# A second timetable for the attention stage of a two-layer trunk: shares, merge, gate, weight splits and loads set to other steps, dense rounds 14 steps on

## The chip, the cores and the metric

The kernel runs on one core of one Trainium2 chip. The metric is device microseconds of one launch, the median of several runs. One more execution was taken with the hardware profiler; all rows of the trace come from it. Engines are named as in the profile: PE (TensorE), DVE (VectorE), ACT (ScalarE), POOL (GpSimd), SP (SyncE, which here only issues DMAs).

## The reference, cut to what matters

Two layers on x (1024 tokens by 1024 channels, float32). Layer 0 is a gated short convolution. Layer 1, which the change is in, is an attention with 16 heads of 64 channels in three dilation groups:

```python
proj = h @ w_in                                   # q, k, v of 3 groups, and z
for g, (window, dilation) in enumerate(((128, 1), (512, 4), (2048, 16))):
    q, k = rms_norm(q), rms_norm(k)
    o, l = dilated_group_attention(q, k, v, bias_g, window, dilation)   # l = log of the softmax's sum
alpha = softmax(stack(lses), axis=0)              # shares of the three groups, per token and head
o = sum(alpha[..., None] * stack(outs))           # merge
y = o * silu(z)                                   # gate
return x + y @ w_out                              # dense
```

## The kernel before, in words

The first four fifths of the span make layer 0 and the projections of layer 1; they write q and k (`qkd`), v (`vd`), silu(z) (`zd`) and the residual (`x1d`) to DRAM. The change does not touch them. The last stage reads these back and works through 24 units: a pair of heads `hp` (0 to 7) by a group `g` (0 to 2).

A unit has 4 steps (g = 0 and 1) or 2 (g = 2), so a pair has 10 and the stage has 80. The last step of pair hp is step 10·hp + 9. The order on each engine is written out by hand: all five engines are under a manual schedule, so each does its instructions in the order in which the Python code issues them. `attention(hp, g)` gives each step a table from lag to pieces of work, and the loop at the end runs, at step k, the pieces of lag 0 of step k, of lag 1 of step k−1, and so on:

- lag 0, `A`: PE scores into two of three PSUM banks, then on DVE bias and row minimum (L935), which frees the banks. `E` (end of the step): ACT exponentials.
- lag 2, `B`: PE transposes (L948), copies from PSUM to `pts` on DVE or ACT.
- lag 4, `C`: PE products with V (L969, L962); when a unit is through, DVE copies the sum to `o` (L984, and L981 for g = 2).
- `store`: minimum and sum of each row go to DRAM (`nld`, L993 and L996) from the POOL queue; for g = 2, `ml` reads the values of the other two groups back (L991), also from POOL, after `nld` has landed.
- For g = 2 of a pair, lags from its last step: `weights` (2) and `shares` (3) on DVE, with one small exponential on ACT; `store_shares` and `spread` (3) send them through DRAM and back, broadcast, into `fb` and `sqacc` (POOL queue); `scale` (8, 9, 10): three 128x1024 products on DVE (L1035); `add` (9, 10): two 128x1024 sums on POOL (L1038); `gate` (12) on DVE (L1041); `high` (12) on ACT and `low` (13) on DVE (L1048) split the result into two float32r parts.

Pair 7 has an ending of its own, which the change leaves as it is.

The output product is done in rounds of two pairs. A round has 16 tiles (8 row blocks by 2 halves of the tokens); a tile is six matmuls of 128x512 (L1129 to L1131) into one bank `pd`, and at the start of the next step DVE adds the bank to `acc` (L1165). One tile goes into one step, at its end. Round r (0 to 2) begins at step 20·(r+1) + LD, with LD = 13; what is left at step 80 goes in pairs into the steps after it. Its weights are read by `fetch` (SP), split by `split` (ACT, L1140) and `split_low` (DVE, L1143). In this text a dense step is one that has such a tile, a plain step one that has none.

Loads for a unit are issued on SP six steps ahead (bias, q, k) and two steps ahead (V). silu(z) of a pair (`sz`, two buffers) is loaded with q and k of g = 2, at step 10·hp + 2. The 16 `residual` loads (256 KB each) fill `acc` at steps 27 to 42.

Of the kernel before, what the change touches and what calls it, by code (L numbers as in the profile page):

```python
# [10 lines left out]
F32 = mybir.dt.float32  # L11
# [8 lines left out]
P = 128  # L20
D = 1024
S = 1024
# [6 lines left out]
HP = H // 2  # L29
# [6 lines left out]
def trunk(ctx: ExitStack, tc: tile.TileContext, a, out):  # L36
    nc = tc.nc
# [60 lines left out]
    def spread(hf, src, pool):  # L98
        cs = slice(hf * HALF, hf * HALF + HALF)
        pb = pool.tile([P, HALF], F32, name="st", tag="st")  # L100
        for j in range(4):
            b = hf * 4 + j
            nc.tensor.transpose(pb[:, j * P:(j + 1) * P], src[:, b:b + 1].to_broadcast([P, P]), ident)
        if src is rtok:
            nc.scalar.activation(R1[:, cs], pb, AF.Copy)
        else:
            mt = ftile()
            mc = mt.rearrange("p (c q) -> p c q", q=32)
            nc.vector.transpose(mc, pb.rearrange("p (c q) -> p c q", q=32))
            nc.vector.tensor_scalar(er2[:, hf * 16:(hf + 1) * 16], mc[:, :, 0], 8.0 * EPS, None, op0=OP.mult)  # L110
# [9 lines left out]
    zd = dram.tile([HP, P, S], F32, name="zd")  # L120
# [14 lines left out]
    with tc.tile_pool(name="wq", bufs=1) as wq, tc.tile_pool(name="sle", bufs=1) as sle, \  # L135
# [11 lines left out]
        def ftile():  # L147
            t = fp.tile([P, HALF], F32, name="f", tag="f", bufs=12)
            return t
# [185 lines left out]
        with tc.tile_pool(name="rp", bufs=1, side="right") as rp, tc.tile_pool(name="cp", bufs=2, side="right") as cp, \  # L335
# [3 lines left out]
            VB, US, TS, SZ = {}, {}, {}, {}  # L339
# [475 lines left out]
    with tc.tile_pool(name="sp", bufs=1, space=PSUM) as sp, tc.tile_pool(name="ptp", bufs=2, space=PSUM) as ptp, \  # L815
# [11 lines left out]
        QK, VS, SZ, y2, part = {}, {}, {}, {}, {}  # L827
        acc = [ap.tile([P, S], F32, name="acc", tag=f"acc{dt}", bufs=1) for dt in range(KT)]

        def loads(hp, g):  # L830
            QK[hp, g] = [ap.tile([P, S], F32, name="qk", tag="qk", bufs=6) for _ in range(2)]
            for i in range(2):
                nc.sync.dma_start(QK[hp, g][i], qkd[hp, g, i])
            if g == 2:
                SZ[hp] = ap.tile([P, S], F32, name="sz", tag="sz", bufs=2)
                nc.sync.dma_start(SZ[hp], zd[hp])

        def load_v(hp, g):
            VS[hp, g] = ap.tile([P, 8, P], F32, name="V", tag="V", bufs=3)
# [23 lines left out]
        def attention(hp, g):  # L863
# [165 lines left out]
            def spread(w):  # L1029
                fb = u["fb", w] = fbp.tile([P, S], F32, name="fb", tag="fb") if w else sqacc  # L1030
                for s, hs in enumerate((lo, up)):
                    nc.gpsimd.dma_start(fb[hs], fd[hp, w, s][None, :].to_broadcast([64, S]))

            def scale(w):
                nc.vector.tensor_tensor(O[hp, w], O[hp, w], u["fb", w], op=OP.mult)  # L1035

            def add(w):
                nc.gpsimd.tensor_tensor(O[hp, 1], O[hp, 1], O[hp, w], op=OP.add)  # L1038
# [22 lines left out]
            def spread_last(hf):  # L1061

                b0, b1, b2 = (scores().rearrange("p a b -> p (a b)") for _ in range(3))
                for w in (2, 1):
                    for r in range(8):
                        for a, b in enumerate((b0, b1)):
                            hs = slice(64 * a + 32 * hf, 64 * a + 32 * hf + 32)
                            nc.tensor.transpose(b.rearrange("p (w i r) -> p w r i", w=2, r=8)[:, w - 1, r],
                                                u["wide", w][hs, r * P:r * P + P], ident[hs, hs])
                mine = ident.rearrange("p (a h i) -> p h a i", a=2, h=2)[:, hf]  # L1070
                for r in range(8):
                    nc.tensor.matmul(b2.rearrange("p (i a r) -> p r a i", a=2, r=8)[:, r],
                                     u["wide", 0][:, r * P:r * P + P], mine, start=True, stop=True)
                u["fb", 0] = b2
                for w in (2, 1):
                    u["fb", w] = [b.rearrange("p (w i r) -> p w i r", w=2, r=8)[:, w - 1] for b in (b0, b1)]

            def last(hf, i):
                h, z = half(hf), SZ[hp][:, half(hf)]
                if i == 0:  # L1080
                    for w in (2, 1):
                        for a, b in enumerate(u["fb", w]):
                            o = O[hp, w][:, h].rearrange("p (i a r) -> p a i r", a=2, r=8)[:, a]
                            nc.vector.tensor_tensor(o, o, b, op=OP.mult)
                    nc.vector.tensor_tensor(O[hp, 0][:, h], O[hp, 0][:, h], u["fb", 0], op=OP.mult)
                elif i == 1:
                    for w in (2, 0):
                        nc.vector.tensor_tensor(O[hp, 1][:, h], O[hp, 1][:, h], O[hp, w][:, h], op=OP.add)
                    nc.vector.tensor_tensor(z, O[hp, 1][:, h], z, op=OP.mult)
                    if hf == 0:  # L1090
                        y2[hp] = [ap.tile([P, S], F32R, name="qk", tag="qk", bufs=6) for _ in range(2)]
                    nc.scalar.activation(y2[hp][0][:, h], z, AF.Copy)
                else:
                    nc.vector.tensor_tensor(y2[hp][1][:, h], z, y2[hp][0][:, h].bitcast(F32), op=OP.subtract)

            steps = []
# [7 lines left out]
            if g == 2:  # L1104
                if hp == HP - 1:
                    steps[-2][3] = steps[-2].pop(LC)
                    end[3] = end.pop(LC)
                    todo = [(2, shares), (2, wide), (3, lambda: spread_last(0)), (3, lambda: last(0, 0)),
                            (3, lambda: last(0, 1))]
                    ending.update(turn=end.pop(LB)[0], weights=weights, spread=spread_last, last=last)  # L1110
                else:
                    todo = [(LB, weights), (3, shares), (3, store_shares), (3, lambda: spread(2)),
                            (3, lambda: spread(1)), (3, lambda: spread(0)), (8, lambda: scale(2)),
                            (9, lambda: scale(1)), (9, lambda: add(2)), (10, lambda: scale(0)),
                            (10, lambda: add(0)), (12, gate), (12, high), (13, low)]
                for lag, f in todo:
                    end.setdefault(lag, []).append(f)
            return steps, prefetch

        LB, LC = 2, 4  # L1120
        LD = 13
        W, ending = {}, {}

        def dense(ps, kts, dt, hf, first, last):
# [37 lines left out]
        def add_sums():  # L1162
            while sums:
                ps, x = sums.pop(0)
                nc.vector.tensor_tensor(x, ps, x, op=OP.add)  # L1165

        steps, at = [], {}
        for un in units:
            st, prefetch = attention(*un)
            at[un] = len(steps), prefetch  # L1170
            steps += st
        begins, extra = {}, {}
        for un, (k, prefetch) in at.items():
            begins.setdefault(max(-1, k - 6), []).extend([prefetch, lambda un=un: loads(*un)])
        tiles = [(dt, hf) for hf in range(2) for dt in range(KT)]

        def when(k, f, *x):
            begins.setdefault(k, []).append(lambda: f(*x))

        for un, (k, prefetch) in at.items():  # L1180
            when(max(0, k - 2), load_v, *un)
        for i, (dt, hf) in enumerate(tiles):
            when(27 + i, residual, dt, hf)
        for r in range(3):
            k0 = at[2 * r + 2, 0][0] + LD
            k = k0
            for i, (dt, hf) in enumerate(tiles):
                late = k >= len(steps)
                name = "pd" if not late else (("pd", "ps"), ("pd", "ps"), ("pd", "pt"), ("pt", "pd"))[
                    min(k - len(steps), 3)][i % 2]  # L1190
                if i >= 14:
                    name = "po"
# [1 line left out]
                                               some((2 * r, 2 * r + 1), dt, hf, name))  # L1194
                k += (i % 2 if i < 13 else 0) if late else 1
        for kt in range(KT):
            k = at[kt // 2 * 2 + 2, 0][0] + LD - 4 + kt % 2 if kt < 6 else len(steps) - 5 + kt % 2
            when(k - 4 - kt % 2, fetch, kt)
            when(k, split, kt)
            when(k + 1, split_low, kt)  # L1200
        when(len(steps), ending["turn"])
        when(len(steps), ending["weights"])
        for f in begins.pop(-1):
# [1 line left out]
        k = 0  # L1205
        while k < len(steps) + LC - 1 or any(x >= k for x in extra):
            add_sums()
            for lag in (0, 1, LC, 3, *range(LC + 1, 15), LB):
                for f in steps[k - lag].get(lag, ()) if 0 <= k - lag < len(steps) else ():
                    f()  # L1210
            for f in steps[k].get("exps", ()) if k < len(steps) else ():
                f()
            for f in extra.get(k, ()):
                f()
            for f in begins.get(k, ()):
                f()
            k += 1
# [94 lines left out]
```

## Time and profile before

| | |
|---|---|
| median of 3 runs | 1976.92 us (1972.67 to 1980.83) |
| the profiled execution, its own time | 1979.19 us |
| its span in the trace | 1977.4 us |
| mean granted clock of TensorE | 0.989 |
| PE busy | 1919.6 us (97%) |
| DVE busy | 1494.7 us (76%) |
| ACT busy | 886.0 us (45%) |
| POOL busy | 847.3 us (43%) |

Busy shares are of the whole span. The attention stage has its first scores at about 1629 us and ends with the span; shares within it are read from windows.

### The profile page before, as it was taken

The numbers are of one execution on the slowest core, as the hardware profiler recorded it, in microseconds if no ns is written. First come the engines' busy times: TensorE is split into PE (matmuls) and PEld (weight loads), VectorE is DVE, ScalarE is ACT, GpSimd is POOL, SyncE is SP. The second block draws the span as 40 slices with busy tenths as digits, with TensorE's granted clock in tenths as the row PEclk, the third lists the DMA queues.
The fourth block names the chain that finished last, engine by engine and source line by source line (L and its number), as shares of the span: only waits on it lengthen the run. The fifth ranks groups of instructions, "written<-read, shape, count | busy, mean of one in ns | idle before, by whom it ended". The sixth has DMA issues, their size and how long they took to land.

```text
span 1977.4 us, 30596 instructions
## 1 busy us (share of the span) xinstructions
PE 1919.6 (97%) x10894; PEld 1558.5 (79%) x10894; DVE 1494.7 (76%) x2769; ACT 886.0 (45%) x2031; POOL 847.3 (43%) x767
## 2 busy tenths in 40 slices
PE   8999999999999999999999999999999998899988
PEld 6888888888888888878877888788888876576767
DVE  6866766666666555798889689868988867888896
ACT  6433333333334453444343443434334338877770
POOL 0366667766665211334434444444434342323330
PEclk9999999999999999999999999999999998998999
DMA  6312232222324575413233232323233257888742
GB/s 192 121 57 88 86 107 75 96 90 82 94 67 158 179 239 165 141 67 122 92 117 118 72 120 103 121 75 128 86 107 107 101 176 226 235 260 237 204 138 86
DMA packets 116777, 253.79 MB, mean 128 GB/s; under 512 B 17598, under 2 KB 22814, under 8 KB 116624
## 3 DMA queue, kind: packets, MB, share of 16 engines
q1 hardware_dynamic: 93280, 176.89, 28.2%
q0 software_dynamic: 23344, 74.95, 11.2%
q8 instruction: 85, 1.39, 0.3%
q14 instruction: 68, 0.56, 0.1%
HBM read 192.53 MB, written 67.64 MB: 132 GB/s over the span
## 4 chain that ended last, share of the span: by engine, by line
PE 77%; DVE 12%; issue 4%; ACT 3%; DMA 3%; POOL 1%; SPq 0%; DVEq 0%; POOLq 0%; ACTq 0%
PE pp L301 17%; PE pp L304 17%; PE pp L303 17%; PE pp L552 3%; PE pp L553 3%; PE pp L551 3%; PE pt L948 3%; DVE ws L165 2%; PE po L969 2%; DVE blkc L716 2%; PE pp L374 1%; PE pp L375 1%; PE pp L376 1%; ACT xs L941 1%; DMA nld<-nl 1%
## 5 line engine op out<-in xcount | busy, mean ns | idle before, releaser
L165 DVE TENSOR_TENSOR ws<-wr,ws 128x512 fp32r<-128x512 f32 x284 | 280.4, 989 | 122.0 <-ACT ws L164 120.6
L164 ACT ACTIVATE ws<-wr 128x512 fp32r<-128x512 f32 x284 | 178.3, 629 | 357.8 <-PE pp L304 232.7
L164 ACT ACTIVATE ws<-sr 128x512 fp32r<-128x512 f32 x272 | 169.9, 629 | 296.5 <-PE pp L304 235.9
L276 POOL TENSOR_TENSOR sr<-wr 128x512 f32<-128x512 f32 x136 | 185.8, 1366 | 261.3 <-DMA wr<-in_wqk 82.9
L165 DVE TENSOR_TENSOR ws<-sr,ws 128x512 fp32r<-128x512 f32 x272 | 225.8, 838 | 72.0 <-ACT ws L164 69.7
L313 DVE TENSOR_TENSOR f<-pp,f 128x512 f32<-128x512 f32 x204 | 139.8, 685 | 92.3 <-PE pp L304 85.6
L941 ACT ACTIVATE xs<-xs,nl 128x256 f32<-128x256 f32 (+2 forms) x384 | 160.3, 423 | 0.7 <-DVE nl L935 0.7
L309 ACT ACTIVATE f<-pp 128x512 f32<-128x512 f32 x228 | 132.5, 581 | 26.9 <-POOL blkc L682 11.6
L671 ACT ACTIVATE f<-f 128x512 f32<-128x512 f32 x96 | 60.7, 632 | 137.7 <-DVE f L313 100.5
L276 POOL TENSOR_TENSOR sr<-wr,sr 128x512 f32<-128x512 f32 x68 | 88.6, 1303 | 71.3 <-issue 48.1
L935 DVE CUSTOM_DVE_ANT_0 xs<-ps,bt 128x256 f32<-128x256 f32 (+2 forms) x384 | 102.2, 325 | 14.9 <-PE ps L922 7.4
L301 PE MATMUL pp<-blkg,ws 128*128 128x512 f32 x272 | 107.3, 394 | 4.1 <-ACT f L309 4.1
L301 PE MATMUL pp<-blkf,ws 128*128 128x512 f32 x272 | 108.5, 399 | 0.7 <-ACT f L309 0.7
L301 PE MATMUL pp<-blka,ws 128*128 128x512 f32 x272 | 107.3, 394 | 1.5 <-ACT f L309 1.5
L301 PE MATMUL pp<-blkb,ws 128*128 128x512 f32 x272 | 107.5, 395 | 0.0
L301 PE MATMUL pp<-blkd,ws 128*128 128x512 f32 x272 | 107.0, 393 | 0.0
L304 PE MATMUL pp<-blkf,ws 128*128 128x512 f32 x272 | 106.3, 391 | 0.0
L304 PE MATMUL pp<-blka,ws 128*128 128x512 f32 x272 | 106.1, 390 | 0.0
L304 PE MATMUL pp<-blkb,ws 128*128 128x512 f32 x272 | 106.0, 390 | 0.0
L304 PE MATMUL pp<-blkd,ws 128*128 128x512 f32 x272 | 106.0, 390 | 0.0
L303 PE MATMUL pp<-blkg,ws 128*128 128x512 f32 x272 | 106.0, 390 | 0.0
L303 PE MATMUL pp<-blkb,ws 128*128 128x512 f32 x272 | 105.9, 390 | 0.0
(341 smaller groups left out, 5284.5 us busy)
## 6 DMA issues: line engine op xcount, KB each, us to landing
wr<-in_conv_w_in SPq DMA_DIRECT2D x128, 256.0 KB, 2.9
wr<-in_wqk SPq DMA_DIRECT2D x96, 256.0 KB, 3.2
qkd<-blkc POOLq DMA_DIRECT2D x48, 512.0 KB, 3.3
qk<-qkd SPq DMA_DIRECT2D x48, 512.0 KB, 5.5
wr<-in_conv_w_out SPq DMA_DIRECT2D x64, 256.0 KB, 3.2
f<-in_x SPq DMA_DIRECT2D x48, 256.0 KB, 3.7
wr<-in_wv SPq DMA_DIRECT2D x48, 256.0 KB, 3.3
vd<-f POOLq DMA_DIRECT2D x48, 256.0 KB, 2.6
```

Of the source, the lines that this page charges most:

```text
L164: nc.scalar.activation(t[:, 0], src, AF.Copy)
L165: nc.vector.tensor_tensor(t[:, 1], src, t[:, 0].bitcast(F32), op=OP.subtract)
L276: nc.gpsimd.tensor_tensor(t, x, y, op=op)
L301: nc.tensor.matmul(ps, w[:, 0, ws], b[:, k, 0], start=new and k == 0, stop=False, skip_group_check=not new)
L303: nc.tensor.matmul(ps, w[:, 0, ws], b[:, k, 1], start=False, stop=False, skip_group_check=not new)
L304: nc.tensor.matmul(ps, w[:, 1, ws], b[:, k, 0], start=False, stop=end and k == 3, skip_group_check=not new)
L309: nc.scalar.activation(t, ps, AF.Copy)
L313: nc.vector.tensor_tensor(m, ps, m, op=OP.add)
L551: nc.tensor.matmul(ps[dt], w[:, 0, ws], b[:, k, 0], start=(q == k == 0), stop=False)
L671: nc.scalar.activation(sq, t, AF.Square)
L935: nc.vector.tensor_tensor_reduce(out=x, in0=flat[s][:, cols], in1=u["bt"][s][:, bs], op0=OP.add, op1=OP.min, scale=-1.0, scalar=3e38, accu ...
L941: nc.scalar.activation(x, x, AF.Exp, bias=nm, scale=-1.0, accum_out=L)
```

## The change

It gives the pieces after a pair's last step other lags, by the pair: `e` is 1 for pairs 0, 2 and 4, 0 for pairs 1, 3 and 5, and −1 for pair 6, which keeps the old lags. It moves the dense rounds one step on, the weight loads and splits some five steps forward for the first six weight rows, silu(z) five steps back, and it spreads the residual loads over steps 3 to 33. With the two weight parts of a row it sets two steps between ACT's and DVE's share, not one.

| piece | step before | step now |
|---|---|---|
| weights, shares of pair hp < 6 | 10hp+11, +12 | 10hp+12, +13 |
| scale, pairs 0, 2, 4 | 10hp+17, 18, 19 | 10hp+19, 20, 21 |
| scale, pairs 1, 3, 5 | 10hp+17, 18, 19 | 10hp+18, 19, 20 |
| add | with the 2nd and 3rd scale | with the 2nd and 3rd scale |
| gate, low, pairs 0, 2, 4 | 10hp+21, 22 | 10hp+23, 24 |
| gate, low, pairs 1, 3, 5 | 10hp+21, 22 | 10hp+22, 23 |
| sz load | 10hp+2 | 10hp+7 |
| residual load i | 27+i | 3+2i |
| fetch, rows 2r and 2r+1 | 20r+25 | 20r+19 |
| split; split_low | 20r+29, 30; 20r+30, 31 | 20r+24, 25; 20r+26, 27 |
| rows 6, 7: fetch; split; split_low | 71; 75, 76; 76, 77 | 69; 74, 75; 76, 77 |
| dense round r | from 20r+33 | from 20r+34 |

```diff
@@ -831,9 +831,10 @@
             for i in range(2):
                 nc.sync.dma_start(QK[hp, g][i], qkd[hp, g, i])
-            if g == 2:
-                SZ[hp] = ap.tile([P, S], F32, name="sz", tag="sz", bufs=2)
-                nc.sync.dma_start(SZ[hp], zd[hp])
+
+        def load_z(hp):
+            SZ[hp] = ap.tile([P, S], F32, name="sz", tag="sz", bufs=2)
+            nc.sync.dma_start(SZ[hp], zd[hp])
@@ -1109,16 +1110,19 @@
-                    todo = [(LB, weights), (3, shares), (3, store_shares), (3, lambda: spread(2)),
-                            (3, lambda: spread(1)), (3, lambda: spread(0)), (8, lambda: scale(2)),
-                            (9, lambda: scale(1)), (9, lambda: add(2)), (10, lambda: scale(0)),
-                            (10, lambda: add(0)), (12, gate), (12, high), (13, low)]
+
+                    e = -1 if hp == HP - 2 else 1 - hp % 2
+                    w = 2 if e < 0 else 3
+                    todo = [(w, weights), (w + 1, shares), (w + 1, store_shares), (w + 1, lambda: spread(2)),
+                            (w + 1, lambda: spread(1)), (w + 1, lambda: spread(0)), (e + 9, lambda: scale(2)),
+                            (e + 10, lambda: scale(1)), (e + 10, lambda: add(2)), (e + 11, lambda: scale(0)),
+                            (e + 11, lambda: add(0)), (e + 13, gate), (e + 13, high), (e + 14, low)]
@@
-        LD = 13
+        LD = 14
@@ -1179,8 +1183,10 @@
             when(max(0, k - 2), load_v, *un)
+            if un[1] == 2:
+                when(k - 1, load_z, un[0])
         for i, (dt, hf) in enumerate(tiles):
-            when(27 + i, residual, dt, hf)
+            when(3 + 2 * i, residual, dt, hf)
@@ -1194,10 +1200,10 @@
-            k = at[kt // 2 * 2 + 2, 0][0] + LD - 4 + kt % 2 if kt < 6 else len(steps) - 5 + kt % 2
-            when(k - 4 - kt % 2, fetch, kt)
+            k = at[kt // 2 * 2 + 2, 0][0] + 4 + kt % 2 if kt < 6 else len(steps) - 6 + kt % 2
+            when(k - 5 - kt % 2, fetch, kt)
             when(k, split, kt)
-            when(k + 1, split_low, kt)
+            when(k + 2, split_low, kt)
@@ -1205,7 +1211,7 @@
-            for lag in (0, 1, LC, 3, *range(LC + 1, 15), LB):
+            for lag in (0, 1, LC, 3, *range(LC + 1, 17), LB):
```

What this does to the queues is seen at three places. The first is DVE in step 51 before, between the dense rounds 0 and 1 (pair 3's gate L1041, pair 4's weights L1005 to L1008, and the lower part of a weight row, L1143, stand in one step):

```order
L984 COPY o<-po 128x512
L1041 TENSOR_TENSOR sz<-o,sz 128x1024
L1005 TENSOR_TENSOR mx<-ml 128x16
L1006 TENSOR_TENSOR mx<-mx,nl 128x16
L1007 TENSOR_TENSOR f<-mx,ml 128x8x4
L1008 TENSOR_TENSOR f<-mx,nl 128x8x2
L1143 TENSOR_TENSOR y_15962<-wraw,y_15962 128x1024
```

In the change (line numbers are up to six higher) the same gate and weights stand in step 52, the weights ahead of the gate, and no weight row is split there:

```order
L1006 TENSOR_TENSOR mx<-ml 128x16
L1007 TENSOR_TENSOR mx<-mx,nl 128x16
L1008 TENSOR_TENSOR f<-mx,ml 128x8x4
L1009 TENSOR_TENSOR f<-mx,nl 128x8x2
L1042 TENSOR_TENSOR sz<-o,sz 128x1024
L860 COPY pts<-pt 128x384
```

The second is where that lower part went: DVE at the end of step 46 and the start of step 47, in the dense round 0.

```order
L860 COPY pts<-pt 128x256
L1147 TENSOR_TENSOR y_15636<-wraw,y_15636 128x1024
L1169 TENSOR_TENSOR acc<-pd,acc 128x512
L936 ISA xs,nl<-ps,bt 128x256
L936 ISA nl 128x1
```

Its neighbours are the additions of dense tiles to `acc`, where before it stood among plain steps.

The third is POOL, from one pair's read of `ml` to the next pair's, before (`o<-o` are the two adds of the pair ahead):

```order
L993 DMA nld<-nl 128x8x4
L996 DMA nld<-nl 512x1x4 x2
L1038 TENSOR_TENSOR o<-o 128x1024
L991 DMA ml<-nld 64x64 x2
L1038 TENSOR_TENSOR o<-o 128x1024
L1027 DMA fd<-fo 64x6x8 x2
```

and in the change:

```order
L994 DMA nld<-nl 128x8x4
L997 DMA nld<-nl 512x1x4 x2
L992 DMA ml<-nld 64x64 x2
L1039 TENSOR_TENSOR o<-o 128x1024 x2
L1028 DMA fd<-fo 64x6x8 x2
```

The first add stood ahead of the read of `ml`, and now both stand behind it, for pairs 0 to 5.

## Rows read from the trace of the kernel before

**Rows 1.** Windows: start:end, length, busy us by engine (instructions), PEclk, DMA share, GB/s.
```profile
1740.00:1760.00 20.00, 20.00 (x245) 15.40 (x246) 15.83 (x63) 13.08 (x54) 6.40 (x10) 1.00 1.05 283
1800.00:1820.00 20.00, 15.45 (x190) 11.48 (x188) 18.58 (x57) 15.53 (x56) 5.02 (x6) 0.74 0.45 150
```

**Rows 2.** Timeline of PE around the gaps between dense rounds: start us, us, instruction [idle before].
```profile
1797.74 0.40 PE L1131 MATMUL po<-y,y 128*128 128x512 f32 x1
...
1809.07 1.23 PE L922 MATMUL ps<-qk 64*64 64x192 f32 x11 [3.19 <-DVE nl L935]
...
1818.28 0.59 PE L1129 MATMUL pd<-y,y 128*128 128x512 f32 x1
...
1876.19 0.47 PE L1129 MATMUL po<-y,y 128*128 128x512 f32 x1
...
1877.42 0.40 PE L1131 MATMUL po<-y,y 128*128 128x512 f32 x1
...
1897.72 0.48 PE L1129 MATMUL pd<-y,y 128*128 128x512 f32 x1
```

**Rows 3.** Waits of DVE, 1621 to 1950 us: waiter, releaser: total, times, longest.
```profile
DVE mx L1005 <- DMA ml<-nld: 6.4, 2, 6.0
DVE o L1035 <- DMA fb<-fd: 2.9, 2, 1.6
DVE sz L1041 <- POOL o L1038: 2.4, 2, 2.1
```

**Rows 4.** Timeline of DVE, steps 50 to 53, between dense rounds 0 and 1.
```profile
1804.69 3.64 DVE L1143 TENSOR_TENSOR y<-wraw,y 128x1024 fp32r<-128x1024 f32 x1 [1.16 <-ACT y L1140]
1808.25 0.41 DVE L935 CUSTOM_DVE_ANT_0 xs<-ps,bt 128x256 f32<-128x256 f32 x1
...
1809.62 0.68 DVE L984 COPY o<-po 128x512 f32<-128x512 f32 x1
1810.23 1.21 DVE L1041 TENSOR_TENSOR sz<-o,sz 128x1024 f32<-128x1024 f32 x1
1811.36 0.16 DVE L1005 TENSOR_TENSOR mx<-ml 128x16 f32<-128x16 f32 x1
...
1811.96 1.22 DVE L1143 TENSOR_TENSOR y<-wraw,y 128x1024 fp32r<-128x1024 f32 x1
...
1814.47 0.19 DVE L1018 TENSOR_TENSOR den<-f,ml 128x32 f32<-128x32 f32 x1
...
1815.53 1.22 DVE L1048 TENSOR_TENSOR y<-sz,y 128x1024 fp32r<-128x1024 f32 x1
...
1818.50 1.94 DVE L981 COPY o<-po 128x512 f32<-128x512 f32 x2
```

**Rows 5.** Timeline of DVE, the copies of g = 2 in steps 13 and 33.
```profile
1669.30 1.89 DVE L981 COPY o<-po 128x512 f32<-128x512 f32 x2
...
1739.34 1.04 DVE L981 COPY o<-po 128x512 f32<-128x512 f32 x1
```

**Rows 6.** Timeline of POOL: stores and reads back of pairs 2 and 4, adds of pairs 1 and 3.
```profile
1716.19 0.71 POOL L996 DMA_DIRECT2D nld<-nl  x1 [4.39 <-ACT xs L941]
...
1726.62 1.08 POOL L991 DMA_DIRECT2D ml<-nld  x2 [3.59 <-DMA nld<-nl]
1727.70 2.89 POOL L1038 TENSOR_TENSOR o<-o 128x1024 f32<-128x1024 f32 x1
...
1795.86 0.71 POOL L996 DMA_DIRECT2D nld<-nl  x1 [5.82 <-ACT xs L941]
...
1803.77 1.08 POOL L991 DMA_DIRECT2D ml<-nld  x2 [3.57 <-DMA nld<-nl]
1804.85 2.38 POOL L1038 TENSOR_TENSOR o<-o 128x1024 f32<-128x1024 f32 x1
```

**Rows 7.** DMA issues, 1620 to 1978 us: count, KB each, median us to landing.
```profile
wraw<-in_wo SPq DMA_DIRECT2D x8, 512.0 KB, 10.6
```

**Rows 8.** Waits of SP's queue, 1600 to 1978 us.
```profile
SPq L836 <- DVE y L1048: 41.8, 5, 12.2
```

## The prediction

> **What bounds the kernel now.** I read the windows of the attention stage first, then PE's timeline where the windows show it idle, then what DVE, on which PE waits there, is doing, and last the queues that DVE waits for.
>
> In a dense step PE is the bound: the window inside dense round 0 has PE busy for all of its 20 us at a granted clock of 1.00, with DVE at 15.8 [rows 1]. Dense round 1 runs from 1818.28 to 1877.42 + 0.40 = 1877.82 without a gap: 59.5 us for 16 tiles and the 15 ordinary step parts between them. A tile takes 1877.82 − 1876.19 = 1.6 us, so the rest of a step takes (59.5 − 25.6) / 15 = 2.26 us, and a dense step 3.86 us [rows 2].
>
> Between rounds 0 and 1 it is different. The window of steps 49 to 53 has PE busy for 15.45 us only, a clock of 0.74 (part of the time at 1.2 instead of 2.4 GHz), and DVE busy for 18.58 [rows 1]. The last tile of round 0 ends at 1797.74 + 0.40 = 1798.14 and round 1 begins at 1818.28: 20.1 us for five step parts that PE alone could do in 5 x 2.26 = 11.3. Between rounds 1 and 2 it is 1897.72 − 1877.82 = 19.9 us. PE's largest idle time there, 3.19 us, ends with DVE's reduction of scores [rows 2]. So plain steps that carry merge work are bound by DVE, and that is where the change can act.
>
> DVE's rows say why [rows 4]. In step 50 it waits 1.16 us for ACT's part of a weight row (L1140), and then the lower part, L1143, takes 3.64 us, where the same form in step 51 takes 1.22. POOL's add starts 0.16 us after it and lasts 2.38 us [rows 6]. Step 51 then holds gate, weights and another weight row.
>
> Before the first dense round every step is plain. From the copies of step 13 to those of step 33 there are 70.0 us for 20 steps [rows 5], against 20 x 2.26 = 45 for PE. The waits that show are 6.0 us in step 11 for `ml`, 2.9 for `fb`, and 2.4 at the gate for POOL's add [rows 3].
>
> **The change part by part.** Times by spacing of starts [rows 4]: four score reductions 1809.62 − 1808.25 = 1.37 us; a copy of `o` 0.61; a 128x1024 product or difference 1.13; `weights` 1811.96 − 1811.36 = 0.60; `shares` 1.06; the two L981 copies 1.94. The addition to `acc` has the copy's size: 0.6. No instruction is added or removed; all terms are waits and cover.
>
> 1. *Between rounds 0 and 1.* From the end of the last tile, now in step 49, DVE does: step 50, acc 0.6, scores 1.37, third scale 1.13, a copy to `pts` 0.6; step 51, scores 1.37, copy of `o` 0.61; step 52, scores 1.37, weights 0.60, gate 1.13, copy 0.6; step 53, scores 1.37, L981 1.94. That is 12.7 us. Shares and `low` come behind L981 and hold nothing that the next tile needs. PE then does C and B of step 54, 1.9 us (a step part less its scores), so the next round starts 14.6 us after; I add 0.3 for `ml` and the gate, whose POOL work ends about when DVE gets there (rival 3 has the working). 14.9 against 20.1 is **−5.2 us**. Bounds: 11.3 (PE alone) gives −8.8; a full repeat of the blocked 2.4 us and another 0.8 at the gate give −2.0.
> 2. *Between rounds 1 and 2.* The same steps 20 later: 14.9 against 19.9, **−5.0 us** (−8.6 to −1.8).
> 3. *The weight rows' new place.* In step 46 DVE now has acc 0.6, scores 1.37, a copy 0.6 and L1143's 1.13: 3.7 us, under the 3.86 of a dense step. This is the cover of the move; ACT's 13.08 of 20 us there [rows 1] leaves room for its part. Step 43 is over it: acc 0.6, scores 1.37, L981 1.94, shares 1.06, gate 1.13 are 6.1 us. The tile of step 44 waits for the addition of step 43's tile (one bank), which comes 6.1 − 3.86 + 0.6 = 2.8 us after that tile instead of within 2.26: 0.5 us, and again in step 63. **+1.0 us** (0 to +3, if steps 44 to 49 catch nothing up).
> 4. *Steps 0 to 33.* `weights` of pair 0 one step later lets DVE do the scores of step 12 before it stops: the 6.0 us shrink by 1.37 to 2.26, say 1.6. The gate two steps later (pair 0) and one later (pair 1) should lose its 2.4 us. `fb` of pair 1 is needed as long after its issue as before, but the weight rows are no longer fetched just ahead of it and seven of the residual loads are gone from there; I take half of the 2.9, 1.4. Against it: `weights` of pair 1 and its gate come at the landing of `ml` and the end of the second add within a microsecond, +1.2. Sum **−4.2 us** (bounds: all that shows as waits, −11.7; on the other side rival 3). Rows 0 and 1 of the weights stay in plain steps, 24 to 27 instead of 29 to 31, at no change; their loads land 10.6 us after issue [rows 7], and five steps of at least 2.26 us cover that by little.
> 5. *SP's queue.* The load of `sz` held the queue for 41.8 us in all, behind `low` of two pairs before [rows 8]; now its buffer is free when it is issued. No PE or DVE wait in the stage names a load of q, k or V, so I cost this at nothing. The same for the residual loads: in steps 3 to 33 the DMA queues take nine more of them.
> 6. *Dense rounds one step on.* Step 33 becomes plain, step 73 too, and one tile goes from step 73 to the steps after 80. PE does the same work; DVE, which is busy throughout that end, gets one more addition (0.6) while PE saves a dense step's tile before it: 0 (−1 to +1.6).
>
> Sum: −5.2 − 5.0 + 1.0 − 4.2 = **−13.4 us**. Against the profiled execution's 1979.2 that is 1965.8; the median of the runs is 2.3 us lower, so 1963.5. A difference of 0.5% (9.9 us) is about what can be told from no change.
>
> **The blocked difference: row and rule.** The row says that a DVE difference with both inputs in SBUF took 3.64 us beside a POOL add and 1.22 without [rows 4, 6], and that another add took 2.89 instead of 2.38 us [rows 6]. The Trainium skill, "SBUF — State Buffer", section "Who interferes with whom", states that a VectorE instruction with two SBUF inputs and a GpSimd instruction that reads SBUF exclude each other, and that the second to issue waits for the whole of the first. The trace agrees on the wait (3.64 − 1.22 = 2.42 us, one add), while by its starts the blocked one was the earlier by 0.16 us. It speaks against this change, since `scale` is such an instruction and the adds have moved: rival 1.
>
> **The rivals.**
>
> *1. The third scale meets the first add.* Both adds now wait behind `ml`. In step 50 `scale` starts 0.6 + 1.37 = 2.0 us after the tile's end, which is about 1798.14 + 3.86 + 2.0 = 1804.0 on the old clock; POOL comes free for its add at 1804.85 [rows 6]. So DVE is ahead by 0.8 us, and a little lateness turns it. Price: 2.4 us for the scale, 0.8 at the gate, in steps 50 and 70, and 2.4 in step 21: 8.8 us, which leaves −4.6: 1972.
>
> *2. DVE's work is only carried about.* If dense steps at 3.7 of 3.86 us do not hold the extra work (waits between engines eat the margin), steps 43 to 49 and 63 to 69 stretch by some 0.5 us each, 7 us, and step 33, now plain with L981, shares and `low`, by 2: −13.4 + 9 is −4.4: 1972.5. For it: DVE at 17 to 18 of 20 us there after the move. Against: PE has no gap at all there now [rows 1].
>
> *3. Slower: the read-back gets longer.* From the store of `nld` to the issue of `ml` POOL took 7.9 us in pair 4's case and 10.4 in pair 2's [rows 6]. Call it T. Gate can go T + 1.1 + 2 x 2.4 = T + 5.9 after the store, as both adds now stand behind `ml`. DVE gets to the gate of pair 3 about 2.2 + 3.86 + 7.7 = 13.8 us after the store, and of pair 1 at about 13.4. So T of 7.9 costs nearly nothing and each further microsecond costs one at pairs 1, 3 and 5, and one each at the `weights` of pairs 0 and 1. Nine residual loads and two weight rows more in steps 3 to 33 are 3.3 MB, at 283 GB/s [rows 1] 12 us of the DMA queues. With T 3.5 us up everywhere the price is 5 x 3.5 = 17.5: slower from there on, 1981. For it: T was 10.4 where DMA was dense. Against: between the rounds the DMA share is 0.45 [rows 1].
>
> **How the numbers follow.** Forecast 0.62, rival 1 0.16, rival 2 0.12, rival 3 0.10. The forecast's own range, with terms 1, 2 and 4 between their nearer bounds, is 1955 to 1971; rivals 1 and 2 lie at 1972, and for no more than 2 in 10 outside I go to 1953 and 1977. Faster by over 0.5% means under 1967.0: 0.54 of the forecast's 0.62 and 0.02 of the others, 0.56. Slower by over 0.5% is the far half of rival 3, 0.07. The rest, 0.37, is within.
>
> **What would show it.** In the changed profile: no lower weight part over 1.3 us; 14 to 16 us between the last tile of a round and the first of the next; PE still without gaps in steps 34 to 49; DVE's wait for `ml` at 4 to 5 us in step 12; gate waits under 1 us. The prediction is wrong if a `scale` takes 3.6 us (rival 1), if dense steps take over 4.1 us (2), or if `nld` to `ml` takes over 11 us (3).

## The result and the profile after

The change takes 1983.01 us (median of 20 runs, 1976.57 to 1986.24) where the kernel before takes 1976.93 (20 runs on the same chip): a ratio of 1.0029, with a 95% interval of 1.0019 to 1.0039. Forecast were 1963.5 us and a range of 1953 to 1977. The change is a little slower, within the 0.5% named as "no change", and the forecast gain of 13.4 us is not there.

The profiled execution of the change took 1977.11 us, near the lowest of its runs. Its stage, from the first scores (1625.94) to the span's end (1975.3), is 349.4 us long; before it was 349.3 (from 1628.13 to 1977.4). That execution lies 5.9 us under its kernel's median and the one of before 2.3 us over, so the rows show the forecast gain missing, but not the 6 us by which the medians differ. The table counts by stretches. Each is from one execution; the first stretch differs by some 4 us between kernels whose order there is nearly the same (116.7 in the change, 117.8, 119.2 and 121.1 in the runs 1, 6 and 7 below, which leave its main causes as they are). The change has one step more ahead of its first tile and one less behind the start of round 2; the last row takes 2.26 us for it, the prediction's figure for a step without its tile.

| us | to the first tile | round 0 | gap | round 1 | gap | from round 2 to the end |
|---|---|---|---|---|---|---|
| before | 110.4 | 59.6 | 20.1 | 59.5 | 19.9 | 79.7 |
| the change | 116.7 | 62.9 | 15.2 | 62.9 | 17.2 | 74.5 |
| difference, step moved taken out | +4.0 | +3.2 | −4.9 | +3.4 | −2.7 | −2.9 |

Both gaps are shorter, as forecast. The stretch ahead of the dense rounds is longer, which was not forecast, and so are both dense rounds, by far more than the 0.5 us each that was. PE's timeline shows where (the same view as [rows 2]; the first two rows are steps 12 and 20, the third step 44 and the last but two step 64):

```profile
1664.73 1.94 PE L949 MATMUL pt<-ident,xs 128*128 128x128 f32 x8 [6.54 <-DVE pts L860]
...
1693.27 1.55 PE L923 MATMUL ps<-qk 64*64 64x192 f32 x14 [7.12 <-DVE nl L936]
...
1782.45 1.20 PE L949 MATMUL pt<-ident,xs 128*128 128x128 f32 x8 [2.87 <-ACT pts L862]
...
1805.10 0.40 PE L1135 MATMUL po<-y,y 128*128 128x512 f32 x1
...
1820.71 0.48 PE L1133 MATMUL pd<-y,y 128*128 128x512 f32 x1
...
1860.58 1.14 PE L949 MATMUL pt<-ident,xs 128*128 128x128 f32 x8 [2.86 <-ACT pts L862]
...
1883.20 0.40 PE L1135 MATMUL po<-y,y 128*128 128x512 f32 x1
...
1900.77 0.48 PE L1133 MATMUL pd<-y,y 128*128 128x512 f32 x1
```

Windows of the change (columns as in [rows 1]): between the rounds PE is busier than before (17.52 against 15.45 of 20 us, at a clock of 1.00 against 0.74), while inside round 0 it now stops, and from 1680 to 1700 the clock is 0.74 where it was 0.98 before.

```profile
1680.00:1700.00 20.00, 12.88 (x182) 9.39 (x182) 12.30 (x58) 11.55 (x56) 6.57 (x7) 0.74 1.00 248
...
1780.00:1800.00 20.00, 17.55 (x182) 13.37 (x183) 15.29 (x58) 15.59 (x51) 6.55 (x11) 0.91 0.70 202
1800.00:1820.00 20.00, 17.52 (x265) 12.88 (x264) 19.44 (x74) 16.09 (x67) 6.11 (x5) 1.00 0.47 160
```

**The stop in a dense round.** ACT's timeline, step 43 into 44: `high` waits for the gate on DVE, and behind it stand the two copies to `pts` that PE waits for. DVE does shares and gate first:

```profile
1780.85 1.06 ACT L1046 ACTIVATE y<-sz 128x1024 fp32r<-128x1024 f32 x1 [3.81 <-DVE sz L1042]
1781.81 1.07 ACT L862 ACTIVATE pts<-pt 128x512 f32<-128x512 f32 x2
```

```profile
1777.67 1.03 DVE L982 COPY o<-po 128x512 f32<-128x512 f32 x1
1778.55 0.18 DVE L1019 TENSOR_TENSOR den<-f,ml 128x32 f32<-128x32 f32 x1
...
1779.47 0.25 DVE L1024 TENSOR_TENSOR fo<-f,mx 128x48 f32<-128x48 f32 x1
1779.60 1.22 DVE L1042 TENSOR_TENSOR sz<-o,sz 128x1024 f32<-128x1024 f32 x1
```

**The stops ahead of the rounds.** DVE's waits, 1640 to 1740 (columns as in [rows 3]): the wait for `ml` is no shorter than before (pair 0's is 6.5 us, it was 6.0), and a new one has come, for the landing of a store of `nld`.

```profile
DVE mx L1006 <- DMA ml<-nld: 8.9, 2, 6.5
DVE xs L936 <- DMA nld<-nl: 7.4, 1, 7.4
```

POOL's timeline shows where it comes from (the view of [rows 6]). Pair 0's share transfers `fb` (1.5 MB with `sqacc`) now go out at 1676.37, after 5.91 us of waiting (the row names PE; `fd`, for which it waits too, landed 0.6 us ahead), and pair 1's three stores of `nld` directly behind them:

```profile
1669.08 1.38 POOL L1028 DMA_DIRECT2D fd<-fo  x2 [10.97 <-DVE fo L1024]
1676.37 2.10 POOL L1033 DMA_DIRECT2D fb<-fd  x4 [5.91 <-PE pt L949]
1678.45 1.03 POOL L1033 DMA_DIRECT2D sqacc<-fd  x2
1679.47 0.92 POOL L994 DMA_DIRECT2D nld<-nl  x1
1680.39 0.78 POOL L997 DMA_DIRECT2D nld<-nl  x1
1681.32 0.71 POOL L997 DMA_DIRECT2D nld<-nl  x1 [0.16 <-issue]
1693.73 1.08 POOL L992 DMA_DIRECT2D ml<-nld  x2 [11.70 <-DMA nld<-nl]
```

Before, the same `fb` went out 4.7 us earlier. The first store stood right behind it there too and took 12.1 us to land (12.9 now), but no wait came of it; the other two were issued later, and the last was read back 8.1 us after its issue, where it is now 1693.73 − 1681.32 = 12.4:

```profile
1671.66 2.10 POOL L1032 DMA_DIRECT2D fb<-fd  x4 [2.40 <-PE ps L917]
1673.75 1.02 POOL L1032 DMA_DIRECT2D sqacc<-fd  x2
1674.76 0.92 POOL L993 DMA_DIRECT2D nld<-nl  x1
...
1683.64 0.71 POOL L996 DMA_DIRECT2D nld<-nl  x1 [4.33 <-ACT xs L941]
...
1691.74 1.08 POOL L991 DMA_DIRECT2D ml<-nld  x2 [4.01 <-DMA nld<-nl]
```

The later start of `fb` has two parts: `fd` is issued later (1669.08, before 1667.87), and it takes 6.1 us to land instead of 2.0. With the shares a step later, `fd` stands behind the loads that SP has just issued; before, `fd` was issued ahead of them:

```profile
1666.41 0.84 SPq L833 DMA_DIRECT2D qk<-qkd  x2
...
1667.83 0.85 SPq L842 DMA_DIRECT2D V<-vd  x2
1668.79 0.78 SPq L837 DMA_DIRECT2D sz<-zd  x1
```

The residual loads are not what makes `fd` slow (5.5 us without them, run 3), and with the shares a step earlier it lands in 2.0 again (run 2). Whether it is the load of `sz`, which the change has put there, or those of q, k and V was not tried.

The chain of waits of the change in this window has the first store as one piece of 12.87 us:

```profile
1679.47 12.87 DMA nld<-nl
1693.27 1.55 PE ps L923 x14
```

### The profile page after: what moved, and what is told of

Read it like the earlier page. It is cut to its first block, busy times and chain, and to the rows that moved or that the text cites. A ratio compares the mean times of both kernels' runs of the same rounds, so it can differ in the third digit from the quotient of the medians.

```text
span 1975.3 us, 30620 instructions
## 1 busy us (share of the span) xinstructions
PE 1910.9 (97%) x10894; PEld 1553.3 (79%) x10894; DVE 1495.4 (76%) x2769; ACT 885.8 (45%) x2031; POOL 848.5 (43%) x767
## 4 chain that ended last, share of the span: by engine, by line
PE 77%; DVE 12%; issue 5%; DMA 3%; ACT 3%; POOL 1%; SPq 0%; DVEq 0%; POOLq 0%; ACTq 0%
PE pp L301 18%; PE pp L304 18%; PE pp L303 17%; PE pp L552 3%; PE pp L551 3%; PE pp L553 3%; DVE ws L165 2%; PE pt L949 2%; PE po L970 2%; DVE blkc L716 1%; PE pp L374 1%; PE pp L375 1%; PE pp L376 1%; DMA nld<-nl 1%; ACT xs L942 1%
## 5 line engine op out<-in xcount | busy, mean ns | idle before, releaser
L301 PE MATMUL pp<-blkg,ws 128*128 128x512 f32 x272 | 107.2, 394 | 3.5 <-ACT f L309 3.5
L301 PE MATMUL pp<-blka,ws 128*128 128x512 f32 x272 | 107.1, 394 | 0.7 <-ACT f L309 0.7
L304 PE MATMUL pp<-blka,ws 128*128 128x512 f32 x272 | 106.0, 390 | 0.0
L303 PE MATMUL pp<-blka,ws 128*128 128x512 f32 x272 | 105.9, 389 | 0.0
```

The source lines that it names most:

```text
L301: nc.tensor.matmul(ps, w[:, 0, ws], b[:, k, 0], start=new and k == 0, stop=False, skip_group_check=not new)
L303: nc.tensor.matmul(ps, w[:, 0, ws], b[:, k, 1], start=False, stop=False, skip_group_check=not new)
L304: nc.tensor.matmul(ps, w[:, 1, ws], b[:, k, 0], start=False, stop=end and k == 3, skip_group_check=not new)
```

## The experiments

Twelve kernels, each against the kernel before on the same chip; the change's own ratio is 1.0029 [1.0019, 1.0039]. All but the eleventh start from the change. Three theories stood at the start. A: the loss lies in holding pair 0's values a step longer (the ring of three `nl` buffers, the later shares). B: the read-back from `nld` to `ml` takes longer, since more transfers share its way. C: the loss lies in the dense rounds, where `high` stands ahead of ACT's copies.

**1. A longer ring.**

```diff
-u["nl"] = sm.tile([P, 8, 4], F32, name="nl", tag="nl", bufs=3)
+u["nl"] = sm.tile([P, 8, 4], F32, name="nl", tag="nl", bufs=5)
```

> The change with five buffers for the row minima nl instead of three. Theory A (the nl ring: the store of pair 1's first unit stands on POOL's queue behind fb, fb behind the landing of fd, and the scores of step 20 wait 7.4 us until that store has landed and its buffer is free): the 7.4 us wait of L936 on nld goes, 1983 becomes 1976 to 1979. Theory B (the DMA queues are fuller in steps 3 to 33, everything that goes through DRAM is late): the wait only moves, to the weights of pair 1 waiting for ml, and the time stays at 1981 to 1984.

Measured: 1984.12 us, 1.0036 [1.0023, 1.0049]. The 7.4 us stop is gone, but DVE's wait for `ml` ahead of the rounds grew from 8.9 to 15.9 us. The ring only decides which instruction waits for the slow landing.

**2. Shares a step earlier again**, for all pairs.

```diff
-                    w = 2 if e < 0 else 3
+                    w = 2
```

> The change with weights and shares of all pairs at the old steps, 10hp+11 and 10hp+12; all else as in the change. Theory A: fd leaves ahead of step 13's work, fb and the store behind it on POOL go out 3 us or more earlier, the wait at step 20 falls from 7.4 to under 4 us, the DVE wait for ml in step 11 is 6 to 8 us, and shares no longer stand ahead of the gate in steps 43 and 63, so the ACT wait for the gate there shrinks by 1 us: 1976 to 1980. Theory B: 1982 to 1985, since the traffic is the same.

Measured: 1988.99 us, 1.0065 [1.0052, 1.0078], 6 us slower than the change, with 13.3 us of waiting for `ml` before the rounds and 4.5 us instead of 7.4 in step 20. The later shares are a gain over all; in the profiled execution it lies in the first gap, round 1 and the end (1.9, 1.5 and 1.6 us), and the first stretch (119.9) is within the spread named above. Theory A falls.

**3. Residual loads at their old steps.**

```diff
-            when(3 + 2 * i, residual, dt, hf)
+            when(27 + i, residual, dt, hf)
```

> The change with the residual loads at steps 27 to 42, as before the change. Theory B: nine loads of 256 KB less in steps 3 to 26; the POOL waits for nld (50.5 us over 7 waits in the change, 25.6 before) fall to 35 us or less and the time to 1975 to 1979. Theory A: the queue order is untouched, the wait at step 20 stays over 5 us: 1981 to 1984.

Measured: 1979.32 us, 1.0016 [1.0005, 1.0027], 3.7 us less than the change by the medians. The `ml` wait of pair 0 fell from 6.5 to 4.1 us; DVE's wait in step 20 stayed (8.1).

**4. High and low a step later.**

```diff
-(e + 11, lambda: add(0)), (e + 13, gate), (e + 13, high), (e + 14, low)]
+(e + 11, lambda: add(0)), (e + 13, gate), (e + 14, high), (e + 15, low)]
```

> The change with high and low one step later than now, the gate where it is. Theory C (in steps 43 and 63 the gate stands behind L982 and shares, ACT waits 3.8 us for it with the copies of the transposes queued behind, and PE stops for 2.9 us in a dense step): both PE gaps go, 5 to 6 us with the clock's return: 1976 to 1978. Rival: DVE itself is the bound there (6.1 us of work in a step of 3.86), and PE stops as long for the scores' banks: 1982 to 1984.

Measured: 1978.00 us, 1.0012 [0.9997, 1.0027], 5.0 less than the change. Both stops of 2.87 and 2.86 us are gone and the rounds take 61.0 and 60.8 us. ACT waits for the gate 2.5 us in all instead of 16.3. Theory C is shown by the stops:

```profile
ACT y L1046 <- DVE sz L1042: 2.5, 3, 0.9
```

The rounds gain 1.8 and 2.0 us, less than the stops, for PE now stops twice in each of them: in the first tile for `low`, which this edit has put a step later, and in steps 44 and 64 for the addition of a tile. The second is the rival's share:

```profile
1753.85 0.50 PE L1134 MATMUL pd<-y,y 128*128 128x512 f32 x1 [1.26 <-DVE y L1049]
...
1791.81 0.50 PE L1133 MATMUL pd<-y,y 128*128 128x512 f32 x1 [0.89 <-DVE acc L1169]
```

**5. The spreads a step after the shares**, so that the next pair's first store goes ahead of them on POOL.

```diff
-(w + 1, store_shares), (w + 1, lambda: spread(2)),
-(w + 1, lambda: spread(1)), (w + 1, lambda: spread(0)),
+(w + 1, store_shares), (w + 2, lambda: spread(2)),
+(w + 2, lambda: spread(1)), (w + 2, lambda: spread(0)),
```

> Only edit: the three spreads (the fb loads) are issued one step after the shares, so on POOL the next pair's first nld store stands ahead of them. Theory D (in the change the fb issues wait 5.9 us on POOL for fd to land, and the next pair's nld stores are queued behind that wait and behind the 1.5 MB of fb transfers): pair 1's nld store is issued near 1675 instead of 1679.5 and lands within 8 us instead of 12.9, the 7.4 us stop in step 20 shrinks to under 3 us, POOL's waits of ml for nld fall from 50.5 us towards the 25.6 us of before; the whole is 4 to 6 us faster than the change, about 1978. Theory E (it is the mass of transfers in those steps, the weight rows of pair 0 and 1 and the residual among them, that slows the landing): the store is issued earlier and lands as late, the stop stays over 5 us, 1982 to 1984. A cost against both: fb lands later and scale(2) waits for it, at most 2 us a pair.

Measured: 1979.84 us, 1.0014 [1.0002, 1.0026], 3.2 less than the change by the medians, but the intervals overlap. The first store lands in 6.4 us instead of 12.9 and the stop in step 20 is gone, but the other two stores still stand behind the transfers, and their read-back takes longer still; DVE now waits 2.8 us for `fb`, 1.6 for `sqacc` and 11.9 for `ml`, 16.3 in all, as much as the change's 7.4 and 8.9:

```profile
1671.57 0.92 POOL L994 DMA_DIRECT2D nld<-nl  x1
1677.74 2.10 POOL L1033 DMA_DIRECT2D fb<-fd  x4 [5.25 <-PE ps L923]
1679.83 1.02 POOL L1033 DMA_DIRECT2D sqacc<-fd  x2
1680.85 1.57 POOL L997 DMA_DIRECT2D nld<-nl  x2
1696.26 1.07 POOL L992 DMA_DIRECT2D ml<-nld  x2 [13.84 <-DMA nld<-nl]
```

So theory D holds for the first store, and the expectations were missed that POOL's waits fall to 25.6 us (51.1) and that the whole is 4 to 6 us faster. That total misled in itself: before, the first add stood ahead of the read of `ml` and filled part of the wait.

**6. Weight rows 0 and 1 five steps later**, about where they were.

```diff
-            k = at[kt // 2 * 2 + 2, 0][0] + 4 + kt % 2 if kt < 6 else len(steps) - 6 + kt % 2
+            k = at[kt // 2 * 2 + 2, 0][0] + (9 if kt < 2 else 4) + kt % 2 if kt < 6 else len(steps) - 6 + kt % 2
```

> Only edit: weight rows 0 and 1 are fetched and split five steps later, about where they were before (rows 2 to 7 stay). Theory E (the 1 MB fetch of rows 0 and 1, issued at 1683.3 while pair 1's nld stores are in flight, makes these land 4 us later): the step-20 stop shrinks from 7.4 to about 3.5 us, the kernel is 3 to 4 us faster than the change, about 1979.5. Theory D (the stores are late because of the wait on POOL and the fb transfers ahead of them): the fetch is issued 4 us after the stores, the stop stays over 6 us, 1982 to 1984.

Measured: 1982.35 us, 1.0033 [1.0019, 1.0047]: not told apart from the change; DVE's wait in step 20 is 8.7 us. Their fetch is not its cause.

**7. The third scale in the second's step.**

```diff
-(e + 10, lambda: add(2)), (e + 11, lambda: scale(0)),
+(e + 10, lambda: add(2)), (e + 10, lambda: scale(0)),
```

> Only edit: the third scale stands in the same step as the second, so it is not issued beside POOL's first addition. The rival about the third scale (it and POOL's addition hold each other up: 3.52 us instead of 1.22 us in the gap of rounds 1 to 2, 2.63 us in that of rounds 0 to 1): the scales of pairs 3 and 5 take about 1.2 us each, the gap of rounds 1 to 2 falls from 17.2 to about 15, that of rounds 0 to 1 from 15.2 to about 14, the kernel is 2 to 3.5 us faster than the change, about 1980. If the addition's work is only moved (two scales in one step stand in front of the copies that ACT and PE wait for): the gaps stay within 1 us, 1982 to 1984.

Measured: 1983.37 us, 1.0035 [1.0021, 1.0049]: no gain. The third scales do take 1.22 us; the first gap is 14.0 instead of 15.2, the second 17.8 instead of 17.2. There the scale now stands ahead of the addition of the round's last tile, which starts 1.2 us after the tile's end, and DVE waits 0.5 us for `ml`: the work is moved, not saved.

**8. Edits 3 and 4 together.**

> Two edits that were shown one by one: high and low one step later, and the residual loads back at steps 27 on. If the two costs are separate (ACT's order in steps 44 and 64, transfers in steps 3 to 33) their gains of 5.0 and 3.7 us add: about 1974.3, below the kernel before by 2 to 3 us. If they are the same time counted twice (the later stages catch up what the first lose): 1977 to 1979, level with the kernel before.

Measured: 1971.37 us, 0.9970 [0.9960, 0.9981]. That is 11.6 us under the change, 3 more than the two gains add to (5.0 + 3.7 gives 1974.3), and this version is faster than both kernels. Taken singly, the runs 3, 4 and 5 have intervals that overlap the change's, so their 3.7, 5.0 and 3.2 us are rough figures; together the first two are clear of it.

**9. Edits 3, 4 and 5 together.**

> Three edits together: spreads one step after the shares, high and low one step later, residual loads back at steps 27 on. If the three costs are separate, their gains against the change (3.2, 5.0 and 3.7 us) add: about 1971, which the run with two edits has already; with the third about 1968. If the spread's gain is only another share of the same waits in steps 3 to 33 that the residual's removal has won already: 1970 to 1972, level with the run with two edits. Either way no stop of over 3 us in step 20.

Measured: 1969.77 us, 0.9961 [0.9946, 0.9977]; not told apart from run 8. The first stretch is 110.9 us, so with the moved step taken out 1.7 us under the kernel before; the second gap is 18.8.

**10. The timetable alone**: residual loads and all weight rows back at their old steps.

```diff
-            k = at[kt // 2 * 2 + 2, 0][0] + 4 + kt % 2 if kt < 6 else len(steps) - 6 + kt % 2
-            when(k - 5 - kt % 2, fetch, kt)
+            k = at[kt // 2 * 2 + 2, 0][0] + 9 + kt % 2 if kt < 6 else len(steps) - 5 + kt % 2
+            when(k - 4 - kt % 2, fetch, kt)
             when(k, split, kt)
-            when(k + 2, split_low, kt)
+            when(k + 1, split_low, kt)
```

> Of the change only the timetable of weights, shares, spreads, scales, additions, gate, high and low is left, with sz's load and the dense rounds 14 steps on; all weight rows and the residual loads are back at their old steps. Compared with the run whose only edit was the residual (1979.3) this gives the price of the rows' new places. If the rows' places cost nothing or little, as that run and the one with rows 0 and 1 say: 1978 to 1981, with the PE stops of 2.87 us in steps 44 and 64 unchanged, since they come from gate and high. If the rows' splits on ACT and DVE in steps 44 to 47 are part of those stops: the stops fall under 1.5 us, about 1975. If the rows' new places are what shortened the gaps between the dense rounds: the gaps are back at 18 to 20 us, 1982 to 1986.

Measured: 1988.22 us, 1.0057 [1.0045, 1.0070]: 8.9 us more than run 3, from which only the rows' places differ. That is more than any of the three cases had. The gaps are back at 20.1 and 21.2 us, against 15.1 and 17.0 in run 3, and in the first of them scale and lower weight part are both held up (DVE):

```profile
1811.83 3.23 DVE L1036 TENSOR_TENSOR o<-o,sqacc 128x1024 f32<-128x1024 f32 x1
...
1815.32 3.32 DVE L1147 TENSOR_TENSOR y<-wraw,y 128x1024 fp32r<-128x1024 f32 x1
```

The shorter gaps come from the rows' new places, as terms 1 and 2 had it. The stops of 2.87 us in steps 44 and 64 stayed: the splits have no part in them.

**11. The kernel before with the early residual loads alone.**

```diff
-            when(27 + i, residual, dt, hf)
+            when(3 + 2 * i, residual, dt, hf)
```

> The kernel before with one part of the change alone: residual loads at steps 3, 5, 7 and so on. The prediction costed this at nothing. If the price seen in the change (3.7 us) is that of 4 MB more in queues that the read-back nld to ml shares, it appears here too: ml's wait in step 12 grows from 6.0 to about 8, 1979.5 to 1981. If it is a price only together with the later shares: 1976 to 1978.

Measured: 1981.10 us, 1.0024 [1.0015, 1.0032]. The loads cost 4.4 us there (1981.10 against 1976.75), some 3.7 in the change. Pair 0's wait for `ml` is 7.6 us instead of 6.0.

**12. Run 9, and pair 6's weights, shares and spreads a step later.**

```diff
-                    w = 2 if e < 0 else 3
+                    w = 3
```

> The run with three edits, and pair 6's weights, shares and spreads one step later, as those of pairs 0 to 5. In the change, shares of pair 6 stand in step 72 on DVE ahead of the gate and of the copy that PE waits for, and wait there for ACT's small exponential; between the dense rounds 0 and 1 the shares stand behind everything that the next round needs. If that is why the gap of rounds 1 to 2 stayed at 17.2 us (18.8 with three edits) where 14.9 was forecast: it falls to 15 to 16.5, and the run is about 2 us under the 1969.8 of the run with three edits, 1967 to 1968.5. If it is the third scale's meeting with POOL's first addition that makes the difference of the two gaps: the gap stays over 17.5, 1969 to 1971, or the pair's end comes later and it is slower.

Measured: 1964.75 us (5 runs, 1964.21 to 1967.85), 0.9942 [0.9929, 0.9956]: 5 us under run 9 and 12 under the kernel before. The second gap fell from 18.8 to 14.2 us, more than expected, since the third scale came clear of POOL's add as well. Why it did is not shown, and may be luck. The first stretch, which this edit does not touch, is 3.3 us shorter in this execution too. DVE and POOL of run 9, then of run 12:

```profile
1877.45 3.75 DVE L1036 TENSOR_TENSOR o<-o,sqacc 128x1024 f32<-128x1024 f32 x1
```

```profile
1877.71 2.39 POOL L1039 TENSOR_TENSOR o<-o 128x1024 f32<-128x1024 f32 x1
```

```profile
1875.44 1.22 DVE L1036 TENSOR_TENSOR o<-o,sqacc 128x1024 f32<-128x1024 f32 x1
```

```profile
1876.05 5.29 POOL L1039 TENSOR_TENSOR o<-o 128x1024 f32<-128x1024 f32 x2
```

Of the 4.5 us, 3.75 − 1.22 = 2.5 are the scale's; that the rest is the shares' moving behind the copy is argued from DVE's order, not tried by itself.

## Why the prediction was wrong

Two steps of it failed most: term 3 looked for the price of the full step 43 on DVE alone, and term 4 had no wait for the landing of pair 1's store, while term 5 put the early residual loads at nothing. In the profiled executions the terms 1, 2, 3, 4 and 6 came to −4.9, −2.7, +6.6, +4.0 and −2.9 us, where −5.2, −5.0, +1.0, −4.2 and 0 were forecast. Their sum is +0.1, and the further 6 us of the medians are in no row shown.

**Term 1, right, with some luck.** Forecast were 14.9 us for the first gap; it is 15.2. No lower weight part takes more than 1.22 us, as was to be seen, and run 10 shows the rows as the cause. But the third scale met the add in part and took 2.63 us instead of 1.22, so the rest of the count must have been about 1 us too long.

**Term 2, half right.** "The same steps 20 later" was not so: pair 6 keeps the old lags, so its shares stand in step 72 ahead of the gate and of a copy that PE waits 2.10 us for, where pair 4's stand behind everything. The third scale took 3.52 us there besides. 14.9 was forecast, 17.2 came; in run 12, where both are gone, it is 14.2. DVE in the change, steps 70 to 72:

```profile
1885.76 3.52 DVE L1036 TENSOR_TENSOR o<-o,sqacc 128x1024 f32<-128x1024 f32 x1
...
1893.63 0.19 DVE L1019 TENSOR_TENSOR den<-f,ml 128x32 f32<-128x32 f32 x1
...
1894.69 1.22 DVE L1042 TENSOR_TENSOR sz<-o,sz 128x1024 f32<-128x1024 f32 x1
1895.83 0.55 DVE L860 COPY pts<-pt 128x384 f32<-128x384 f32 x1
```

**Term 3, wrong in size and in engine.** "0.5 us, and again in step 63" asked only what DVE's 6.1 us do to the bank of the tile. DVE did need about that (0.89 us in each round of run 4, where it stands alone), but the longer way to PE led over ACT: `high` stands in ACT's order right behind the gate, and two copies behind `high`. The rounds are 3.2 and 3.4 us longer, 6.6 where +1.0 was forecast; run 4, which takes the ACT path out, is 5.0 us faster by the medians, 3.9 by its rounds. The working never asked who stands behind `high` on its engine.

**Term 4, wrong in sign.** −4.2 was forecast for steps 0 to 33; +4.0 came in the profiled execution, and more in its variants. DVE's waits for DMA and POOL in this stretch say which parts failed: they were 11.9 us in all before and are 16.3 now. The gate's 2.4 us and the 2.9 for `fb` are gone, as forecast or better. Two parts failed.

The first is pair 0's wait for `ml`, which was to shrink by 1.6 us and did not. That is the residual loads, against "so I cost this at nothing. The same for the residual loads" in term 5: with them at their old steps the wait is 4.1 to 4.5 us (runs 3, 8, 9, 10 and 12), the forecast 4 to 5; with them early it is 5.8 to 7.2 (the change and the runs 1, 4, 5, 6 and 7). Over the whole kernel they cost 4.4 us in run 11, which is clear of noise.

The second is the stop of 7.4 us in step 20, for which the term had nothing. Pair 1's first store lands late behind `fb`, and `fb` goes out later because the shares, a step later, send `fd` behind SP's loads. Run 5 shows that the place behind `fb` makes this stop; it does not show what the stop cost, since `ml` then came later and nothing clear was won. In run 9 this stretch is 1.7 us shorter than before and in run 12, with the same order there, 5.0, so the gain forecast seems to have been there and covered; one execution of each does not prove it.

**Term 5** was right on SP's queue: its waits of `sz` fell from 41.8 [rows 8] to 11.8 us and no gain came of it. It was wrong on the residual loads. Whether the new place of `sz`'s load has a price of its own, by the landing of `fd`, no run shows.

**Term 6.** 0 was forecast; from round 2 on the change is 2.9 us shorter, the moved step taken out. What gives this was not tried.

**The rivals.** Rival 1 happened in the second gap (3.52 us beside the add) and in part in the first (2.63), but its price was not on the path alone: run 7 removes both, wins 1.2 us in the first gap and nothing in all. Rival 2 did not come: without ACT's stop (run 4) the rounds of 61 us are 1.3 to 1.4 over before, two short stops of PE each, where it had 3.5 us. Rival 3 is the nearest: its sign was right and its mark, over 11 us from `nld` to `ml`, was passed (12.4). It laid this to fuller queues everywhere, but only pair 1 is over 11 us, and there the stores stand behind `fb` on POOL's own queue; pair 2's fell from 10.4 to 6.7. What it said of the residual loads holds: they lengthen the wait for `ml`.

## What to carry to other kernels

When an instruction is moved on an engine that works in a fixed order, ask what it waits for there and then list what stands behind it: the 3.8 us that ACT waited for a gate stopped PE for 2.9, by two copies behind it. A small store that another pair waits for lands late when it stands behind a large transfer in the same queue (12.9 us, ahead of it 6.4), so see when the large one starts and what its own start waits for. Loads that nobody waits for can still cost, here 4.4 us, when such stores and their reads are under way. When rounds are taken for alike, look for the one pair that the table treats otherwise.

## What was not expected of the hardware

A DVE product with both inputs in SBUF and a POOL add held each other up depending on tenths of a microsecond. In four places (the change, run 8, run 4 and run 9) where the product started 0.04, 0.15, 0.16 and 0.26 us before the add, it took 3.52, 3.65, 3.64 and 3.75 us; in two (the runs 12 and 8) where it was 0.61 and 0.63 us ahead, 1.22; where it came 0.86 us after the start of the add (the change), 2.63. The Trainium skill, "SBUF — State Buffer", section "Who interferes with whom", has the one that issues first keep the shared pair for its whole length. The traces agree that the loser waits until the other is through. But the starts in the profile do not tell who was first: in the kernel before, a lower weight part that started 0.51 us ahead of the add still took 3.98 us, one that started 0.54 us ahead took 1.21, and in run 7 products that started 0.17 to 0.31 us ahead, each right behind another product, took 1.22 while the add took 3.14 us or more.

```profile
1884.38 3.98 DVE L1143 TENSOR_TENSOR y<-wraw,y 128x1024 fp32r<-128x1024 f32 x1 [1.34 <-ACT y L1140]
```

```profile
1884.89 2.38 POOL L1038 TENSOR_TENSOR o<-o 128x1024 f32<-128x1024 f32 x1
```

TensorE's granted clock followed the stops: 0.74 in the window of the stop in step 20 (0.98 before), and back from 0.74 to 1.00 in the first gap, where PE's idle time shrank. What a stop costs by this, beside its own length, was not measured apart.
